# Seven block products in four of eight pairs, inner features in three parts, and low parts added by transfers: an encoder trunk on one core

## The chip, the cores and the metric

The kernel runs on one core of a Trainium2 chip. TensorE (PE in the profile; PEld is its weight load) multiplies, VectorE (DVE) and ScalarE (ACT) work elementwise, GpSimd (POOL) and SyncE (SP) issue transfers among other things. The metric is the device time of one execution in microseconds.

## The reference

Two layers over a sequence of 256 positions with 2048 features, in float32. Layer 0 mixes by a convolution module and a gating unit, layer 1 by a Fourier transform. Behind each stands the same feed-forward block, and these two blocks are where the change lies:

```
def swiglu(h, w_gate, w_up, w_down):
    return (jax.nn.silu(h @ w_gate) * (h @ w_up)) @ w_down

    h = rms_norm(x, ffn_norm_g[layer])
    x = x + swiglu(h, ffn_w_gate[layer], ffn_w_up[layer], ffn_w_down[layer])
```

`w_gate` and `w_up` are 2048 x 5632, `w_down` is 5632 x 2048.

## The kernel before

**Precision.** A product is done with operands in a rounded format (F32R) and each operand in two parts, a rounded high part and the rest. Weights come from HBM in chunks of 128 x 1024 (512 KB) into `raw` tiles. `parts_of` makes the two parts: ACT copies the chunk into the high part (L130), DVE subtracts that from the chunk (L131). A product takes three matmuls: high by high, high by low, low by high (`three`, L416).

**The feed-forward block.** The 5632 inner features are done in 11 groups of 512. `hidden_group` computes one group's gate and up values for both blocks of 128 positions, over the 16 feature tiles taken as eight pairs. `SEQ` says how a pair is done: "c" is the plain way, eight block products (24 matmuls of 512 columns); "s" is a scheme with seven products (21 matmuls) from sums of weights and of inputs. An "s" pair needs four prepared chunks out of two loaded ones (kinds "1122", "21", "sum", "sum2" in `load`), so it costs DVE additions (L161, L166, L167) besides the splits. `SEQ` is "ccscscsc", so a group has 5 x 24 + 3 x 21 = 183 matmuls. At the end of the last "s" pair ACT copies the shared sum `p1` out of PSUM (L461) and DVE forms the other sums (L462 to L465). `activate` then adds these to the plain sums, takes the sigmoid and multiplies.

The groups are done in two parts (`HALVES` = 6 and 5 groups). After each part the down projection adds that part's product to the residual `res`. For the group that has just ended, `turned` transposes the activations (L495): inside a part between the second and the third pair of the next group, at the end of a part after `PARTIAL` - 1 column tiles of the down projection have been done over the earlier groups.

**Order.** Each engine runs its instructions in the order in which the program has them after a scheduler has placed them. `Weights.chunk` prepares chunks ahead: as long as less than `AHEAD` units of PE work are prepared, it emits another. Small tasks (`activate` and the like) are emitted by ticks, one a chunk. The SP queue issues the loads in order, each once its `raw` tile is free. There are 5 `raw` tiles, 12 `part` tiles and 53 `op` tiles.

Of the kernel before, what the change touches and what calls it, by code (L numbers as in the profile page):

```python
# [22 lines left out]
F32 = mybir.dt.float32  # L23
# [5 lines left out]
P = 128  # L29
# [11 lines left out]
NG = D // GD  # L41
NV = CD // 512
CH = 8
AHEAD = 5
RAWS, PARTS = 5, 12
NOP = 53
HALVES = (6, 5)
SEQ = "ccscscsc"
PARTIAL = 3
NMISC = 3  # L50
PAIRS = 11
OPEN = 5
# [16 lines left out]

_ffn = []  # L70
for _g in HALVES:
    for _c, _ in ORDER * _g:
        _ffn += ["1122", "21", "sum", "sum2"] if _c == "s" else ["w", "w"]
    _ffn += ["w"] * (KD * 4 * _g // CH)
KINDS = (["w"] * ((4 * KD * KC + 2 * KC * KD) // CH) + _ffn + ["w"] * (KD * KD // CH) + _ffn)
UNITS = {"w": 2, "1122": 1, "21": 0.5, "sum": 1, "sum2": 1}
RMS_EPS = 1e-6
LN_EPS = 1e-5

# [11 lines left out]
def trunk(ctx, tc, xT, vec, sgu_gb, sgu_bs, sgu_wT, w, dft_c, dft_s, out):  # L91
# [27 lines left out]
    class Weights:  # L119
        def __init__(self):  # L120
            self.loaded, self.fetched, self.ahead, self.ready = 0, 0, 0, []
            self.tick, self.tasks, self.later, self.credit = 0, [], [], 0.0

        def parts_of(self, x, pieces=1):
# [18 lines left out]
        def load(self, pieces=1):  # L143
            kind = KINDS[self.loaded]
            h = slice(0, 512), slice(512, 1024)
            if kind == "w":
                r = self.parts_of(self.fetch(pieces), pieces)
            elif kind == "1122":
                self.pair = self.fetch(), self.fetch()
                r = self.parts_of(self.pair[0])  # L150
            elif kind == "21":
                x, t = self.pair[1], part()
                nc.scalar.copy(t[:, h[0]], x[:, h[1]])  # L153
                nc.vector.tensor_sub(t[:, h[1]], x[:, h[1]], t[:, h[0]].bitcast(F32))
                r = t,
            elif kind == "sum":

                t = self.sums = raws.tile([P, CH * P], F32, name="raw")
                two = lambda x: x.rearrange("p (o c) -> p o c", o=2)
                b12 = self.pair[1][:, h[0]].rearrange("p (o c) -> p o c", o=1).broadcast_to([P, 2, 512])  # L160
                nc.vector.tensor_add(two(t), two(self.pair[0]), b12)  # L161
                r = self.parts_of(t)
            else:

                t = raws.tile([P, CH * P], F32, name="raw")
                nc.vector.tensor_add(t[:, h[0]], self.sums[:, h[0]], self.pair[0][:, h[1]])  # L166
                nc.vector.tensor_add(t[:, h[1]], t[:, h[0]], self.pair[1][:, h[1]])  # L167
                r = self.parts_of(t)
            self.ahead += UNITS[kind]
            self.loaded += 1  # L170
            self.ready.append((kind, r))
# [23 lines left out]

        def chunk(self):
            while self.loaded < len(KINDS) and (not self.ready or
                                                self.ahead - UNITS[self.ready[0][0]] < AHEAD):
                self.load()
            self.step()  # L200
            kind, r = self.ready.pop(0)
            self.ahead -= UNITS[kind]
            return r
# [265 lines left out]
    def activate(norm, cs, sums, out):  # L469

        for b in range(NB):
            g, u = sums[2 * b:2 * b + 2]
            if b == 0:
                nc.vector.tensor_add(g, cs[0], g)  # L474
            else:
                nc.vector.tensor_sub(g, cs[2], g)
            nc.vector.tensor_add(u, cs[2 * b + 1], u)
        yield 1, 2.8
        for b in range(NB):
            g, u = sums[2 * b:2 * b + 2]  # L480
            r = norm.r[:, b:b + 1]
            sg = op(F32)
            nc.scalar.activation(sg, g, AF.Sigmoid, scale=r)  # L483
            nc.vector.scalar_tensor_tensor(g, g, r, sg, op0=ALU.mult, op1=ALU.mult)
            nc.vector.scalar_tensor_tensor(g, u, r, g, op0=ALU.mult, op1=ALU.mult)
            out.append(g)
        yield 1, 2.8

    def turned(h, hs, from_misc):

# [10 lines left out]
    def ffn(norm, after, last=False):  # L501
# [9 lines left out]
        for half, n in enumerate(HALVES):  # L511
# [13 lines left out]
                weights.start(activate(norm, cs, sums, h))  # L525
            k = 4 * (n - 1)
            accs = []
            for m in range(PARTIAL):
                if m == PARTIAL - 1:
                    turned(h, hs, True)  # L530
                accs.append(product(hs[:k], last=False))
            for m in range(KD):
# [1 line left out]
                    acc, = products(hs, 1)  # L534
                    nc.vector.tensor_add(res[:, m, :], res[:, m, :], acc)
                else:
                    x = residual(m, product(hs[k:], accs[m], first=False) if m < PARTIAL else product(hs))
                if final:
                    after(m, res[:, m, :])

# [79 lines left out]

    ys = []
    for j in range(KC):
        ys.append(op(F32, (P, S + 2 * PAD)))
        nc.gpsimd.memset(ys[j][:, :PAD], 0.0)
        nc.gpsimd.memset(ys[j][:, PAD + S:], 0.0)

# [4 lines left out]


    vs = [[[op() for _ in range(NV)] for _ in range(2)] for _ in range(NB)]
    vg = [[op(F32) for _ in range(NV)] for _ in range(NB)]
    st = small.tile([P, NB, NV, 6], F32, name="bnst")

    def gate_norm(nb, accs):
# [159 lines left out]
    weights.drain()  # L797

    n2 = Norm("mix1")
    ffn(n1, n2.add)  # L800


# [126 lines left out]
def _feed_forward(gate, up, down):  # L929
# [4 lines left out]
    for n in HALVES:  # L934
# [6 lines left out]
                chunks += [np.concatenate([t[:, g] for t in x], axis=1) for x in two]  # L941
        h = down[4 * g0:4 * (g0 + n)].transpose(2, 0, 1, 3)
        k = 4 * (n - 1)
        t = [h[:PARTIAL, :k], h[:PARTIAL, k:], h[PARTIAL:]]
        chunks += list(_chunks(np.concatenate([x.reshape(-1, P, P) for x in t])))
        g0 += n
    return np.stack(chunks)
# [63 lines left out]
```

## Time and profile before

| | |
|---|---|
| median of three runs | 1876.99 us (1874.48 to 1878.91) |
| the profiled execution | 1877.13 us, its span 1875.0 us |
| PE busy | 1849.9 us (99% of the span) |
| DVE busy | 1532.4 us (82%) |
| ACT busy | 1052.6 us (56%) |
| POOL busy | 19.8 us (1%) |

The span runs from the first to the last instruction of the program. A matmul's shown duration reaches beyond the start of the next, so PE's rate is read from the distance of starts, not from the mean duration. ACT, DVE and the transfers work beside PE, and a time of theirs counts only where PE waits for it.

### The profile page before, as it was taken

Reading aid. Unit: us, or ns where it says so; the run is one execution under the profiler, and the core shown is the slowest. Engines: PE = TensorE matmul, PEld = TensorE weight load, DVE = VectorE, ACT = ScalarE, POOL = GpSimd, SP = SyncE. Lnnn points to the kernel's source line nnn. Section 1 sums busy time; section 2 is a strip of 40 time slices with the busy share of each in tenths; the row PEclk is TensorE's granted clock in tenths of the full one; section 3 lists DMA queues with packets and bytes.
Section 4 is the critical chain, followed back from the end, with each engine's and each line's share of the span. In section 5 each row is a group of like instructions: output and inputs, shape, how many; then the busy total and the mean of one; then the engine's idle time right before and its main releaser. Section 6 shows DMA issues by size and latency. Waiting matters only on the chain.

```text
span 1875.0 us, 26253 instructions
## 1 busy us (share of the span) xinstructions
PE 1849.9 (99%) x9802; PEld 1584.6 (85%) x9802; DVE 1532.4 (82%) x2061; ACT 1052.6 (56%) x1444; POOL 19.8 (1%) x46
## 2 busy tenths in 40 slices
PE   8999999999999999999999999999999999999997
PEld 7989988878888888888888988888888888888886
DVE  7999969999997557899876678989997558999854
ACT  8988745555554335555555655555554335555642
POOL 1000000000000000000000000000000000000000
PEclk9999999999999999999999999999999999999999
DMA  7544553555557545555655264555556555555752
GB/s 269 174 165 151 180 191 135 185 197 202 180 205 251 188 164 181 180 196 197 242 196 185 70 212 147 191 183 205 205 208 222 190 169 180 191 188 200 252 188 83
DMA packets 98312, 351.38 MB, mean 187 GB/s; under 512 B 11268, under 2 KB 12420, under 8 KB 98184
## 3 DMA queue, kind: packets, MB, share of 16 engines
q1 hardware_dynamic: 97464, 347.73, 53.6%
q8 instruction: 77, 1.26, 0.3%
q10 hardware_dynamic: 720, 1.97, 0.3%
q14 instruction: 51, 0.42, 0.1%
HBM read 347.54 MB, written 2.10 MB: 186 GB/s over the span
## 4 chain that ended last, share of the span: by engine, by line
PE 86%; DVE 6%; DMA 4%; issue 2%; ACT 2%; SPq 0%; POOL 0%; POOLq 0%; DVEq 0%; ACTq 0%
PE acc L416 25%; PE acc L323 23%; PE m L416 13%; PE acc L324 12%; DMA raw<-in_w 4%; PE acc L333 2%; PE acc L334 2%; PE acc L335 2%; DVE part L131 1%; ACT part L130 1%; DVE raw L161 1%; PE acc L671 1%; PE acc L672 1%; PE acc L673 1%; DVE raw L166 1%
## 5 line engine op out<-in xcount | busy, mean ns | idle before, releaser
L130 ACT CAST part<-raw 128x1024 fp32r<-128x1024 f32 (+1 forms) x725 | 747.8, 1047 | 598.8 <-PE acc L323 288.1
L131 DVE TENSOR_TENSOR part<-raw,part 128x1024 fp32r<-128x1024 f32 (+1 forms) x725 | 872.3, 1219 | 242.1 <-ACT part L130 227.0
L323 PE MATMUL acc<-op,part 128*128 128x512 f32 x1900 | 664.0, 394 | 0.5 <-DVE op L343 0.5
L416 PE MATMUL acc<-part,op 128*128 128x512 f32 x2622 | 648.3, 391 | 0.9 <-ACT part L130 0.4
L416 PEld LDWEIGHTS acc<-part,op 128*128 128x128 f32 x2622 | 488.4, 188 | 108.3 <-ACT part L130 4.4
L324 PE MATMUL acc<-op,part 128*128 128x256 f32 x1900 | 531.9, 280 | 0.0
L323 PEld LDWEIGHTS acc<-op,part 128*128 128x128 f32 x1900 | 355.7, 187 | 82.1 <-DVE op L343 0.8
L416 PE MATMUL m<-part,op 128*128 128x512 f32 x1404 | 364.6, 391 | 0.5 <-DVE op L465 0.5
L324 PEld LDWEIGHTS acc<-op,part 128*128 128x128 f32 x1900 | 359.0, 189 | 0.5
L416 PEld LDWEIGHTS m<-part,op 128*128 128x128 f32 x1404 | 262.3, 188 | 56.9 <-DVE part L131 1.1
L333 PE MATMUL acc<-op,part 128*128 128x256 f32 x404 | 117.2, 290 | 6.5 <-ACT part L130 5.1
L335 PE MATMUL acc<-op,part 128*128 128x256 f32 x404 | 115.1, 286 | 1.2 <-DVE part L131 1.2
L334 PE MATMUL acc<-op,part 128*128 128x256 f32 x404 | 115.8, 287 | 0.0
L161 DVE TENSOR_TENSOR raw<-raw 128x1024 f32<-128x1024 f32 x66 | 80.7, 1222 | 10.7 <-DMA raw<-in_w 10.7
L333 PEld LDWEIGHTS acc<-op,part 128*128 128x128 f32 x404 | 78.6, 195 | 7.3 <-ACT part L130 5.5
L335 PEld LDWEIGHTS acc<-op,part 128*128 128x128 f32 x404 | 78.1, 194 | 1.9 <-DVE part L131 1.9
L334 PEld LDWEIGHTS acc<-op,part 128*128 128x128 f32 x404 | 78.8, 195 | 0.3 <-DVE op L232 0.2
L562 ACT ACTIVATE op<-op,vt 128x256 f32<-128x256 f32 x168 | 71.8, 499 | 0.0
L386 DVE TENSOR_TENSOR l<-acc,res 128x256 f32<-128x256 f32 x90 | 38.0, 423 | 32.0 <-PE acc L324 32.0
L153 ACT CAST part<-raw 128x512 fp32r<-128x512 f32 x66 | 41.1, 623 | 27.2 <-DMA raw<-in_w 12.2
L483 ACT ACTIVATE op<-op,is_r 128x512 f32<-128x512 f32 x44 | 31.9, 725 | 43.3 <-DVE op L474 33.1
L579 DVE TENSOR_TENSOR op<-op 128x512 f32<-128x512 f32 x80 | 54.1, 690 | 2.1 <-ACT op L562 1.8
(152 smaller groups left out, 1126.8 us busy)
## 6 DMA issues: line engine op xcount, KB each, us to landing
raw<-in_w SPq DMA_DIRECT2D x655, 512.0 KB, 4.3
res<-in_xT SPq DMA_DIRECT2D x7, 256.0 KB, 7.1
out<-res ACTq DMA_DIRECT2D x3, 512.0 KB, 2.8
raw<-in_w SPq DMA_DIRECT2D x4, 128.0 KB, 3.2
op<-in_sgu_wT SPq DMA_DIRECT2D x2, 256.0 KB, 4.9
raw<-in_dft_s SPq DMA_DIRECT2D x1, 512.0 KB
res<-in_xT SPq DMA_DIRECT2D x2, 128.0 KB, 2.2
raw<-in_dft_c SPq DMA_DIRECT2D x1, 256.0 KB, 2.8
```

The source lines that it names most:

```text
L130: nc.scalar.copy(hi[:, c], x[:, c])
L131: nc.vector.tensor_sub(lo[:, c], x[:, c], hi[:, c].bitcast(F32))
L153: nc.scalar.copy(t[:, h[0]], x[:, h[1]])
L161: nc.vector.tensor_add(two(t), two(self.pair[0]), b12)
L323: nc.tensor.matmul(acc, wh, x, start=first and k == 0, stop=False)
L324: nc.tensor.matmul(acc[:, :S], wl, x[:, :S], start=False, stop=last and k == len(xs) - 1)
L333: nc.tensor.matmul(acc, wh, x[:, :S], start=k == 0, stop=False)
L334: nc.tensor.matmul(acc, wh, x[:, S:], start=False, stop=False)
L335: nc.tensor.matmul(acc, wl, x[:, :S], start=False, stop=k == len(xs) - 1)
L416: nc.tensor.matmul(acc, x[f], wt[e], start=first and i == 0, stop=last and i == 2)
L562: nc.scalar.activation(t[:, f * S:(f + 1) * S], src, AF.Copy, scale=wc)
L579: nc.vector.tensor_add(sums, sums, t)
```

## The change

`SEQ` becomes "ccscsssc": four plain pairs, four with seven products. The parts are 4, 4 and 3 groups. In four of a group's eight plain chunks (`ADDED`, those of the third and fourth plain pair) the low part is made without DVE: ACT copies the chunk into the high part, writes the negative of the high part into the low part, and a transfer issued from POOL adds the chunk to it. `Silu` takes the place of sigmoid and one multiplication. The lead is 7 units from the first feed-forward block on; there are 7 `raw`, 14 `part` and 46 `op` tiles, and two sets of tiles of layer 0 move from `op` to `part` tiles.

```diff
-RAWS, PARTS = 5, 12
-NOP = 53
-HALVES = (6, 5)
-SEQ = "ccscscsc"
-PARTIAL = 3
+AHEAD, AHEAD_FFN = 5, 7
+RAWS, PARTS = 7, 14
+NOP = 46
+HALVES = (4, 4, 3)
+ADDED = (4, 5, 6, 7)
+SEQ = "ccscsssc"
+PARTIAL = lambda n: 3 if n > 3 else 4
...
+            elif kind == "added":
+
+                raw, hi, lo = self.fetch(), part(), part()
+                nc.scalar.copy(hi, raw)
+                nc.scalar.activation(lo, hi.bitcast(F32), AF.Copy, scale=-1.0)
+                nc.gpsimd.dma_start(lo, raw, accum_op=ALU.add)
+                r = hi, lo
...
-                                                self.ahead - UNITS[self.ready[0][0]] < AHEAD):
+                                                self.ahead - UNITS[self.ready[0][0]] < self.lead):
...
-            nc.scalar.activation(sg, g, AF.Sigmoid, scale=r)
-            nc.vector.scalar_tensor_tensor(g, g, r, sg, op0=ALU.mult, op1=ALU.mult)
-            nc.vector.scalar_tensor_tensor(g, u, r, g, op0=ALU.mult, op1=ALU.mult)
+            nc.scalar.activation(sg, g, AF.Silu, scale=r)
+            nc.vector.scalar_tensor_tensor(g, u, r, sg, op0=ALU.mult, op1=ALU.mult)
...
-            for m in range(PARTIAL):
-                if m == PARTIAL - 1:
+            for m in range(PARTIAL(n)):
+                if m == PARTIAL(n) - 1:
...
-        ys.append(op(F32, (P, S + 2 * PAD)))
+        if j % 3 == 0:
+            three_ys = wts.tile([P, 3, S + 2 * PAD], F32, name="part")
+        ys.append(three_ys[:, j % 3, :])
...
-    vg = [[op(F32) for _ in range(NV)] for _ in range(NB)]
+    vg = [wts.tile([P, NV, 512], F32, name="part") for _ in range(NB)]
+    vg = [[t[:, n, :] for n in range(NV)] for t in vg]
...
+    weights.lead = AHEAD_FFN
     ffn(n1, n2.add)
```

The first place is ACT at the end of a hidden group. Before, in the third group of the first block, its queue has these rows; L130 and L153 are copies into high parts, L461 is the copy of `p1`, and the rows behind it are the last chunk of the "s" pair and the chunks of the last plain pair and of the next group:

```order
L153 CAST part_4811<-raw_4799 128x512 [waits DMAHW1_49,PE_49,Activation_49]
L130 CAST part_4816<-raw_4814 128x1024 [waits DVE_49,PE_49,Activation_49]
L461 COPY op_4890<-acc_4691 128x512 [waits PE_49]
L130 CAST part_4823<-raw_4820 128x1024 [waits DVE_49,Activation_49]
L130 CAST part_4841<-raw_4839 128x1024 [waits DMAHW2_49,Activation_49]
L130 CAST part_4859<-raw_4857 128x1024 [waits DMAHW3_49,Activation_49]
L130 CAST part_4880<-raw_4878 128x1024 [waits DMAHW4_49,Activation_49]
L130 CAST part_4901<-raw_4899 128x1024 [waits DMAHW5_49,PE_49,Activation_49]
L130 CAST part_4919<-raw_4917 128x1024 [waits DMAHW6_49,PE_49]
```

In the changed kernel (its line numbers are other ones: L134 and L164 the copies, L472 the copy of `p1`, L155 and L156 the copy and the negation of an added chunk) the same place in the second group reads:

```order
L164 CAST part_4460<-raw_4448 128x512 [waits DMAHW1_49,PE_49,Activation_49]
L472 COPY op_4559<-acc_4349 128x512 [waits PE_49]
L134 CAST part_4468<-raw_4466 128x1024 [waits DVE_49]
L134 CAST part_4481<-raw_4478 128x1024 [waits DMASW3_49,DVE_49]
L155 CAST part_4493<-raw_4491 128x1024 [waits DMAHW2_49]
L156 ACTIVATE part_4494<-part_4493 128x1024 [waits Activation_49]
L155 CAST part_4509<-raw_4507 128x1024 [waits DMAHW3_49]
L156 ACTIVATE part_4510<-part_4509 128x1024 [waits Activation_49]
L134 CAST part_4528<-raw_4526 128x1024 [waits DMAHW4_49]
```

Two of the last "s" pair's copies now stand behind the copy of `p1` instead of one, and behind them the copy and negation of both chunks of the last plain pair, ahead of the next group's first chunk (`part_4528`). 17 of the 22 groups have these rows. In the other five (the first group of each later part, and of the second block) the two copies and the first L155 stand ahead of L472.

The second place is PE at the same end of a group. Before, in the second group, the last product into `p1` (`acc_4325`) is followed by 11 products and then these rows, in which the last plain pair (`part_4475`, `part_4476`) begins:

```order
L416 MATMUL acc_4327<-part_4450,op_4011 128x512
L416 MATMUL m_4205<-part_4457,op_3522 128x512 [waits Activation_49]
L416 MATMUL acc_4328<-part_4457,op_4010 128x512
L416 MATMUL acc_4203<-part_4475,op_3809 128x512 [waits Activation_49]
L416 MATMUL m_4205<-part_4458,op_3522 128x512 [waits DVE_49]
L416 MATMUL m_4205<-part_4457,op_3522 128x512
L416 MATMUL acc_4328<-part_4458,op_4010 128x512
L416 MATMUL acc_4328<-part_4457,op_4011 128x512
L416 MATMUL m_4204<-part_4475,op_3809 128x512
L416 MATMUL acc_4203<-part_4476,op_3809 128x512 [waits DVE_49]
```

In the changed kernel the rows are these; `part_4494` is the low part that a transfer completes (the wait on DMASW), `part_4528` the next group's first chunk. The row of `part_4528` with its wait on ACT is the 22nd after the last product into `p1`, the row with DMASW the 25th:

```order
L427 MATMUL acc_4352<-part_4481,op_4083 128x512
L427 MATMUL acc_4227<-part_4493,op_3802 128x512 [waits Activation_49]
L427 MATMUL m_4228<-part_4493,op_3802 128x512
L427 MATMUL m_4229<-part_4493,op_3802 128x512
L427 MATMUL m_4230<-part_4493,op_3802 128x512
L427 MATMUL acc_4604<-part_4528,op_3617 128x512 [waits Activation_49]
L427 MATMUL acc_4605<-part_4528,op_3617 128x512 [waits DVE_49]
L427 MATMUL acc_4606<-part_4528,op_3617 128x512 [waits DVE_49]
L427 MATMUL acc_4227<-part_4494,op_3802 128x512 [waits DMASW6_49]
L427 MATMUL acc_4227<-part_4493,op_3802 128x512
```

Four products with the high part and three of the next group now stand ahead of the first product with the low part, which waits for a transfer instead of DVE. In the 17 groups these distances are 22 or 23 and 24 to 26 (where a part ends, the 23rd is the down projection's first product), in the five 21 or 23 and 24 or 25. The second low part is waited for nine products further on. Over the program, the hidden groups have 180 products each in place of 183, POOL issues 88 such transfers, and ACT has one more activation table load, ahead of the first `Silu`. The down projection before has two column tiles of 4 x (n - 1) steps ahead of `turned` for a part of n groups (40 steps for six), and now two of 12 for four groups and three of 8 for three.

## Rows read from the trace of the kernel before

**Rows 1.** The page: busy time, share of the span, instructions
```profile
PE 1849.9 (99%) x9802; PEld 1584.6 (85%) x9802; DVE 1532.4 (82%) x2061; ACT 1052.6 (56%) x1444; POOL 19.8 (1%) x46
```

**Rows 2.** Groups by line: form, count, busy us, mean ns, idle
```profile
L416 PE MATMUL acc<-part,op 128*128 128x512 f32 x2622 | 648.3, 391 | 0.9 <-ACT part L130 0.4 <-DVE op L465 0.2
L131 DVE TENSOR_TENSOR part<-raw,part 128x1024 fp32r<-128x1024 f32 (+1 forms) x725 | 872.3, 1219 | 242.1 <-ACT part L130 227.0 <-PE acc L416 8.6 <-PE m L416 0.2
L130 ACT CAST part<-raw 128x1024 fp32r<-128x1024 f32 (+1 forms) x725 | 747.8, 1047 | 598.8 <-PE acc L323 288.1 <-DMA raw<-in_w 90.8 <-DVE raw L161 85.0
L161 DVE TENSOR_TENSOR raw<-raw 128x1024 f32<-128x1024 f32 x66 | 80.7, 1222 | 10.7 <-DMA raw<-in_w 10.7
L166 DVE TENSOR_TENSOR raw<-raw 128x512 f32<-128x512 f32 x66 | 45.5, 690 | 0.7
L484 DVE SCALAR_TENSOR_TENSOR op<-op,is_r 128x512 f32<-128x512 f32 x44 | 32.7, 751 | 0.0
L389 DVE TENSOR_TENSOR res<-acc,l 128x256 f32<-128x256 f32 x106 | 44.8, 424 | 2.6
L364 POOL TENSOR_TENSOR is_r<-is_v,mhalf 128x2 f32<-128x2 f32 x14 | 16.7, 1192 | 1844.9 <-DVE is_v L362 1844.9
L612 ACT ACT_TABLE_LOAD x2 | 2.6, 1283 | 0.0
```

**Rows 3.** Chain that ended last: start us, us, what
```profile
308.53 10.90 PE acc L416 x48
```

**Rows 4.** Timeline of PE, transposes after the second pair: start us, us
```profile
363.06 0.38 PE L495 MATMUL acc<-ident,op 128*128 128x128 f32 x2
494.21 0.44 PE L495 MATMUL m<-ident,op 128*128 128x128 f32 x2
1201.51 0.38 PE L495 MATMUL acc<-ident,op 128*128 128x128 f32 x2
1202.65 0.82 PE L495 MATMUL acc<-ident,op 128*128 128x128 f32 x6
1330.39 0.38 PE L495 MATMUL m<-ident,op 128*128 128x128 f32 x2
```

**Rows 5.** Timeline of ACT at the end of a group
```profile
864.67 0.59 ACT L461 COPY op<-acc 128x512 f32<-128x512 f32 x1 [2.48 <-PE acc L416]
865.15 2.94 ACT L130 CAST part<-raw 128x1024 fp32r<-128x1024 f32 x3
```

**Rows 6.** Waits: engine line <- releaser: us in total, times, longest
```profile
ACT op L461 <- PE acc L416: 21.1, 17, 3.0
```

**Rows 7.** Loads at L139; queue line; small transfers: count, KB, us to landing
```profile
DMA to landing us min/median/max: 2.6/4.3/7.9
q1 hardware_dynamic: 97464, 347.73, 53.6%
op<-op SPq DMA_DIRECT2D x8, 2.0 KB, 1.7
```

**Rows 8.** Windows on either side of the second normalization: busy times, PEclk
```profile
1028.00:1031.00 3.00, 1.51 (x12) 1.31 (x10) 2.27 (x4) 1.94 (x4) 0.00 (x0) 1.00 0.58 221
1031.00:1034.50 3.50, 3.50 (x18) 3.50 (x19) 3.11 (x9) 1.61 (x5) 0.74 (x1) 0.53 0.64 192
1034.50:1038.00 3.50, 3.50 (x30) 3.50 (x30) 1.36 (x3) 1.96 (x7) 0.00 (x0) 0.98 0.71 267
```

**Rows 9.** Timeline of PE there
```profile
1028.94 0.50 PE L370 MATMUL m<-oneD,ssq 128*128 128x2 f32 x4
1030.93 0.78 PE L370 MATMUL m<-oneD,sq 128*128 128x2 f32 x4 [1.49 <-ACT sq L254]
```

**Rows 10.** Timelines of PE and DVE after the first part's last group
```profile
568.06 0.28 PE L324 MATMUL acc<-op,part 128*128 128x256 f32 x1
572.30 0.28 PE L324 MATMUL acc<-op,part 128*128 128x256 f32 x1
576.90 1.41 DVE L485 SCALAR_TENSOR_TENSOR op<-op,is_r 128x512 f32<-128x512 f32 x2
```

More of the change, by code (lines that the diff above doesn't have):

```diff
@@ L43 @@
 CH = 8
-AHEAD = 5
-RAWS, PARTS = 5, 12
-NOP = 53
-HALVES = (6, 5)
-SEQ = "ccscscsc"
-PARTIAL = 3
+AHEAD, AHEAD_FFN = 5, 7
[5 more added lines that the diff above has]
+PARTIAL = lambda n: 3 if n > 3 else 4
 NMISC = 3
@@ L71 @@
 for _g in HALVES:
-    for _c, _ in ORDER * _g:
-        _ffn += ["1122", "21", "sum", "sum2"] if _c == "s" else ["w", "w"]
+    for _i, (_c, _) in list(enumerate(ORDER)) * _g:
+        _k = 2 * SEQ[:_i].count("c")
+        _ffn += (["1122", "21", "sum", "sum2"] if _c == "s" else
+                 ["added" if _k + _j in ADDED else "w" for _j in range(2)])
     _ffn += ["w"] * (KD * 4 * _g // CH)
 KINDS = (["w"] * ((4 * KD * KC + 2 * KC * KD) // CH) + _ffn + ["w"] * (KD * KD // CH) + _ffn)
-UNITS = {"w": 2, "1122": 1, "21": 0.5, "sum": 1, "sum2": 1}
+UNITS = {"w": 2, "added": 2, "1122": 1, "21": 0.5, "sum": 1, "sum2": 1}
 RMS_EPS = 1e-6
@@ L121, in __init__ @@
             self.loaded, self.fetched, self.ahead, self.ready = 0, 0, 0, []
+            self.lead = AHEAD
             self.tick, self.tasks, self.later, self.credit = 0, [], [], 0.0
@@ L482, in activate @@
             sg = op(F32)
-            nc.scalar.activation(sg, g, AF.Sigmoid, scale=r)
-            nc.vector.scalar_tensor_tensor(g, g, r, sg, op0=ALU.mult, op1=ALU.mult)
-            nc.vector.scalar_tensor_tensor(g, u, r, g, op0=ALU.mult, op1=ALU.mult)
+            nc.scalar.activation(sg, g, AF.Silu, scale=r)
+            nc.vector.scalar_tensor_tensor(g, u, r, sg, op0=ALU.mult, op1=ALU.mult)
             out.append(g)
-        yield 1, 2.8
+        yield 1, 1.4
     def turned(h, hs, from_misc):
@@ L536, in ffn @@
                 else:
-                    x = residual(m, product(hs[k:], accs[m], first=False) if m < PARTIAL else product(hs))
+                    x = residual(m, product(hs[k:], accs[m], first=False) if m < PARTIAL(n) else product(hs))
                 if final:
@@ L943, in _feed_forward @@
         k = 4 * (n - 1)
-        t = [h[:PARTIAL, :k], h[:PARTIAL, k:], h[PARTIAL:]]
+        m = PARTIAL(n)
+        t = [h[:m, :k], h[:m, k:], h[m:]]
         chunks += list(_chunks(np.concatenate([x.reshape(-1, P, P) for x in t])))
```

## Prediction

> **What bounds the kernel now.** I read the page first: PE has work for 99% of the span [rows 1], so what counts is the number of products and the moments at which PE waits. The chain of work that ended last gives a product's price: 48 products of 512 columns take 10.90 us [rows 3], 0.227 us each (the 391 ns in the groups by line [rows 2] reach into the next product). The timeline gives a hidden group's price by the transposes that each group has behind its second pair. Three groups lie between 363.06 and 494.21 and three between 1201.51 and 1330.39 [rows 4]: 43.7 us a group in the first block, 43.0 in the second. 183 products take 41.5, and eight transposes 0.9 (two more each time cost 0.11 a piece: x6 lasts 0.82, x2 lasts 0.38), 42.4 in all. So a group loses 1.3 and 0.6 us, at most 21 us over the 22 groups.
>
> Where PE loses that I read from ACT. In 17 of 22 groups ACT stands at L461 waiting for PE to finish `p1`, up to 3.0 us [rows 6]: ACT is ahead of its work, and yet everything behind the copy in its queue can't start before `p1` ends. The timeline shows it: after 2.48 us of idle time the copy starts, and 0.48 us later the casts follow [rows 5]. ACT's share (56%) and DVE's (82%) [rows 1] say little about this place; the order of ACT's queue after `p1` does.
>
> **What the change takes away.** Three products a group are 66 in all, 66 x 0.227 = 15.0 us. Of the 21 us of losses I take off 8, because the waits at the end of the groups are priced anew below and those elsewhere may stay (bounds 0 and 21).
>
> **What lies beside PE.** ACT gets four negations a group (4 x 1.05, the price of a cast [rows 2]) and the casts of a fourth "s" pair; DVE is relieved of four subtractions of 1.22 and two multiplications of 0.75 [rows 2], 6.4 us, and gets 4.5 for the fourth "s" pair (additions of 1.22, 0.69 and 0.69, one subtraction of 1.22 and half a one). Both stay below the time that a group takes, by the shares of [rows 1]. A third part brings 32 residual additions a block at 0.42 [rows 2], also DVE's. The table load takes 1.28 us of ACT once [rows 2]. I cost all these at nothing; what they hide behind is the products of the group. The layer 0 tiles that move to another pool likewise: nothing, give or take 2 us.
>
> **Part ends.** Before, 40 steps of the down projection stand between a part's last group and `turned`. Twelve of them lie between 568.06 and 572.30 [rows 10], so a step takes 0.353 us, and the 40 take 14.1; now there are 24, 8.5 us. The activations were ready about 10.5 us after the part's last group (567.8 to 576.90 + 1.41 [rows 10]); with one multiplication less for each block of positions, 1.4 us sooner: 9.1. So 0.6 us at six places, 3 us with rounding down (bounds 0 and, without the gain of `Silu`, 12).
>
> **The end of a group.** This decides. I count from the start of the last product into `p1`. It takes 0.39 [rows 2], then come ACT's copy (next start 0.48 later [rows 5]) and casts, whose starts lie 0.95 apart (three in 2.94, the last 1.05 long [rows 5]). By the order after the change, in 17 groups: first cast 0.87, second 1.82, high part of the first added chunk 2.77 to 3.82, its negation, which reads the high part, 3.82 to 4.87, second high part 4.77, its negation 5.82, and the next group's first cast only 6.77 to 7.82. PE wants that cast 22.5 products on, at 5.1 us, so **it waits 2.7 us however fast the transfers are**. It wants the low part 25 products on, at 5.67. With L from the issue of the transfer to PE, the low part is there at 4.87 + L, and the two waits overlap: the group loses the larger of 2.7 and L - 0.8. The second low part (6.87 + L, nine products later) asks for the same and adds nothing. In the five other groups the negation runs at 0.87 to 1.92, and the loss is 1.92 + L - 5.67 = L - 3.75.
>
> **The size of L.** No row shows such a transfer. It moves 512 KB as a load does; loads take 2.6 at the least, 4.3 in the median and 7.9 at most [rows 7], under traffic that shares the engines. It also has to read the other summand: 8 packets of 4 KB an engine, at 0.165 us each (53.6% of 16 engines' 1875 us over 97464 packets [rows 7]), 1.3 us. And POOL has to issue it: a small operation there takes 1.19 [rows 2]. That gives 2.6 + 1.3 + 1.2 = 5.1 by the quickest load and 6.8 by the median one. The lower bound is a tiny transfer inside the chip, 1.7 us [rows 7], with 1.3 us of packets and nothing for POOL: 3.0; the upper is the slowest load, 7.9 + 1.3 + 1.2 = 10.4. I take 5.7: nearer 5.1, since a 2-column operation on POOL is not a mere issue.
>
> Then 17 groups lose 4.9 each, 83.3 us, and five lose 1.95, 9.8 us.
>
> **The clock.** In the windows around the second normalization [rows 8] PE has only twelve matmuls within 3 us, eight of them of 2 columns, with 1.49 us of idle time between these [rows 9]; just behind that the granted clock falls to 0.53 of full speed, the lower of its two levels, for 3.5 us, which costs 0.47 x 3.5 = 1.6 us. A pause of 4.9 us, which is broken by a few products, resembles that. I let it cost 1.6 in half of the 17 groups, 14 us (bounds 0 and 27).
>
> **Sum.** Against the profiled execution, 1877.1 us (span 1875.0 and 2.1 around it; the median of the runs is 1877.0, the same): 1877.1 - 15.0 - 8 + 3 + 83.3 + 9.8 + 14 = **1964 us**, slower by 87.
>
> **The rivals.**
>
> *The transfer is quick (L up to 3.5).* Then only the next group's cast is waited for, 17 x 2.7 = 46 us. With little clock loss, 1877.1 - 15.0 - 8 + 46 = 1900, and 1890 to 1910 with the bounds of the vanished waits and of the part ends. For it: tiny transfers take 1.7. Against it: the engines carry loads more than half the time. Chance 0.18.
>
> The Trainium skill, "DMA: Bandwidth & Descriptors", section "Anatomy of one DMA — SWDGE (gpsimd) path", fits a transfer issued from GpSimd by 2.0 us and its bytes over 436 GB/s; for 512 KB that is an estimate of 3.2 us, and by it the time would be this rival's. No run here shows it, and the loads' median of 4.3 for the same bytes [rows 7] lies above it.
>
> *The transfer is slow (L of 8 and more).* The loads' longest times already reach 7.9 [rows 7] while DVE and the queue are busy, as they are at the end of a group. With L = 8: 17 x 7.2 + 5 x 4.25 = 144 us, and with the clock's 27, 1877.1 - 23 + 3 + 144 + 27 = 2028; the case spans 2005 to 2080 (the upper bound of L, 10.4, gives the end). Chance 0.18.
>
> The Trainium skill, "SBUF — State Buffer", section "SBUF: two separate sides", speaks for this one: a transfer issued from GpSimd can sit waiting while DVE holds the port that the two share, because its descriptors aren't written. No run here shows it.
>
> *Faster: PE doesn't stand still at the end of a group.* The saving of 23 us is used up once a group loses 23 / 22 = 1.05 us. For less, ACT's seven steps from `p1` to the next group's cast have to end by 6.2 us instead of 7.82, each one 0.23 us shorter, and L has to be under 1.85. For it: a negation reads and writes rounded numbers and may be quicker than the casts in the rows. Against it: two negations of no length at all take 2 us off the cast, but leave L, and the smallest transfer shown has 1.7. If it held in full, 1877.1 - 23 = 1854. Chance 0.06.
>
> *No change.* The gain and the waits cancel; the same mechanism at 1.05 us a group. Chance 0.02.
>
> **Range and chances.** The forecast's own case is L from 4 to 7. L = 4 gives 1877.1 - 23 + 17 x 3.2 + 5 x 0.25 = 1910, L = 7 with most of the clock's loss 1877.1 - 23 + 3 + 105 + 16 + 25 = 2003. It has the rest, 0.56. From 1890 to 2020 all of it and the quick transfer lie inside, and about a third of the slow one: 0.80. A difference of over 0.2% (3.8 us) is what runs of this kernel can tell. Faster has 0.06, the same 0.02, slower 0.92.
>
> **What would show it.** In the profile after, PE's idle time before the products of the feed-forward block should have two releasers that are almost absent now: the transfers of the added chunks, and ACT's plain cast, once a group, near its end; the waits should come in 17 long ones of about 5 us and five short ones. The new transfers' issue to landing should be 4 to 7 us. ACT should wait at the copy of `p1` (now L472) as before. The page's row of the granted clock should dip once a group where the pauses are long. Distances of transposes three groups apart should be near 3 x (40.9 + 0.9 + 4.9) = 140 us instead of 131.2 and 128.9 (where no part ends in between). The step that I doubt most is L; if PE's idle time at the added low parts is near nothing and the time still grows, the order of ACT's queue was right and L too large. If PE doesn't wait for ACT's cast either, the counting from `p1` is wrong, and the time falls.

## The result, and the profile after

The changed kernel takes 2023.45 us (median of 4 runs, 2019.97 to 2032.56) against 1876.51: the ratio is 1.0785 (95% interval 1.0764 to 1.0805), 147 us slower. The direction was forecast, the size was not: 1964 was predicted, and the time lies 3 us above the range. The profiled execution has a span of 2022.7 us.

The page of the changed kernel: the engines [rows 1], the queues of the transfers [rows 7], and the new transfers (KB each, us from issue to landing):

```profile
PE 1895.1 (94%) x9728; PEld 1596.2 (79%) x9728; DVE 1528.6 (76%) x2117; ACT 1151.6 (57%) x1579; POOL 94.8 (5%) x134
...
q1 hardware_dynamic: 97464, 347.73, 48.7%
q0 software_dynamic: 12672, 46.14, 12.1%
...
part<-raw POOLq DMA_DIRECT2D x88, 512.0 KB, 5.8
```

No engine became the bound by its share: ACT's busy time grew by 99 us and its share by one point, DVE's stayed, and PE's share fell. PE's busy time rose by 45 us although it has 66 products fewer, which points to a lower clock.

The view of cores (mean granted clock), and of the waits of the changed kernel (total us, times, longest):

```profile
core 0: 2022.7 us, clock 0.969
```

```profile
ACT op L494 <- DVE op L485: 116.1, 16, 7.8
...
DVE op L485 <- PE acc L427: 92.7, 17, 6.0
...
PE acc L427 <- DMA part<-raw: 70.1, 24, 4.3
ACT op L472 <- PE acc L427: 51.6, 21, 3.7
...
PE acc L427 <- ACT part L134: 22.3, 28, 1.5
...
PE acc L334 <- ACT part L134: 8.6, 6, 1.4
...
PE m L427 <- ACT part L134: 3.7, 16, 0.3
```

PE stands still for 70.1 us for the transfers and for 22.3 + 8.6 + 3.7 = 34.6 us for ACT's casts, 104.7 us together. The mean clock, 0.969 against 0.997 before, stands for 0.031 x 2022.7 - 0.003 x 1875 = 57 us. With the 15.0 us of products saved that is 104.7 + 57 - 15 = 147 us, as much as the difference of the spans (2022.7 - 1875.0 = 147.7). The sum closes because two inaccuracies of 12 us cancel. Some 12 us of the low clock fall into the waits themselves, where they cost nothing (0.79 over 3.4 us in the windows below, 17 times), so the clock costs about 45. And by the distance of starts each of the 74 waits is 0.16 us longer than shown (a product is shown with 0.39 and costs 0.227), so the waits cost about 116.

One group shows where. Its timeline on PE, from the transposes that begin it to those of the next group (start us, us, idle time before):

```profile
420.41 1.03 PE L505 MATMUL m<-ident,op 128*128 128x128 f32 x8
...
443.54 0.73 PE L427 MATMUL m<-part,op 128*128 128x512 f32 x2 [0.26 <-ACT part L134]
444.49 0.50 PE L427 MATMUL acc<-part,op 128*128 128x512 f32 x1 [0.21 <-ACT part L134]
...
449.49 0.50 PE L427 MATMUL acc<-part,op 128*128 128x512 f32 x1 [1.44 <-ACT part L134]
...
453.72 7.56 PE L427 MATMUL acc<-part,op 128*128 128x512 f32 x21 [3.27 <-DMA part<-raw]
...
471.10 1.03 PE L505 MATMUL acc<-ident,op 128*128 128x128 f32 x8
```

The group takes 50.7 us where its 180 products and eight transposes need 41.8; it loses 8.9. All of it lies at the end: short waits for the last "s" pair's casts, 1.44 for the next group's cast, 3.27 for the low part, and then 21 products that take 7.56 us instead of 4.9. The windows of that stretch (busy us of PE, PEld, DVE, ACT, POOL, then PEclk, DMA share, GB/s) say why these are slow, as [rows 8] do for one place of before:

```profile
446.00:450.30 4.30, 2.86 (x12) 1.86 (x11) 3.05 (x5) 4.27 (x6) 1.72 (x2) 1.00 0.98 281
450.30:453.70 3.40, 0.15 (x1) 0.00 (x0) 3.02 (x3) 1.98 (x3) 0.00 (x0) 0.79 1.07 219
453.70:459.40 5.70, 5.68 (x14) 4.47 (x15) 0.58 (x1) 0.00 (x0) 0.00 (x0) 0.53 0.84 266
459.40:465.00 5.60, 5.60 (x27) 4.60 (x26) 5.60 (x8) 2.89 (x4) 0.00 (x0) 1.00 0.38 145
```

While PE stands still the granted clock falls, and for 5.7 us behind the wait it stays near the lower of its two levels: 14 products where 27 fit into the next 5.6 us. The transfer engines are full (0.98 and 1.07) while the low part is under way. POOL's issues, and the transfers' time from issue to landing (min/median/max), are these for all 88; then the landing for the two of one third plain pair (issued from 369.6) and for the two of the last plain pair of the group shown (from 446.8), of which PE waits for the first, 6.9:

```profile
L157 POOL DMA_DIRECT2D part<-raw x88: 859/859/1042, 318.4 to 1930.4; - x88
DMA to landing us min/median/max: 4.5/5.8/8.0
...
DMA to landing us min/median/max: 5.1/5.4/5.7
...
DMA to landing us min/median/max: 6.9/7.1/7.4
```

The share of the engines doesn't tell the two places apart: in the third pair's window, 369.6 to 374.6, it is 0.98 too. The loads issued in the 6 us ahead differ, two there and four here; no run varies them alone:

```profile
L143 SPq DMA_DIRECT2D raw<-in_w x2: 327/328/328, 365.0 to 368.6; - x2
...
L143 SPq DMA_DIRECT2D raw<-in_w x4: 327/328/328, 442.2 to 445.9; - x4
```

One thing ties the groups together. DVE's L485 adds the sum into which the low part's products go, ACT's L494 (`Silu`) reads the result, and both stand in their engines' queues ahead of work for the next group:

```profile
409.07 0.72 ACT L494 ACTIVATE op<-op,is_r 128x512 f32<-128x512 f32 x1 [7.39 <-DVE op L485]
...
446.77 0.86 POOL L157 DMA_DIRECT2D part<-raw  x1 [23.24 <-ACT part L156]
...
458.82 0.69 DVE L485 TENSOR_TENSOR op<-acc,op 128x512 f32<-128x512 f32 x1 [5.50 <-PE acc L427]
...
459.55 0.72 ACT L494 ACTIVATE op<-op,is_r 128x512 f32<-128x512 f32 x1 [7.27 <-DVE op L485]
```

From L494 it is 37.7 us to the issue of the transfer, 7.0 more until PE uses the low part, 5.1 for the products at the low clock and 0.7 for L485: 50.5 us, the length of a group. A late low part holds ACT for 7.27 us, and that delays the chunks from which the next low part comes. This is read from the rows of one group; e18 below fits it.

### The profile page after: what moved, and what is told of

The parts are those of the page before. It is cut to its first block, busy times and chain, and to the rows that moved or that the text cites. A ratio compares the mean times of both kernels' runs of the same rounds, so it can differ in the third digit from the quotient of the medians.

```text
span 2022.7 us, 26508 instructions
## 1 busy us (share of the span) xinstructions
PE 1895.1 (94%) x9728; PEld 1596.2 (79%) x9728; DVE 1528.6 (76%) x2117; ACT 1151.6 (57%) x1579; POOL 94.8 (5%) x134
## 3 DMA queue, kind: packets, MB, share of 16 engines
q0 software_dynamic: 12672, 46.14, 12.1%
## 4 chain that ended last, share of the span: by engine, by line
PE 73%; DMA 10%; issue 9%; DVE 5%; ACT 2%; POOL 0%; SPq 0%; POOLq 0%; DVEq 0%; ACTq 0%
PE acc L334 22%; PE acc L427 19%; PE acc L335 11%; PE m L427 9%; DMA part<-raw 7%; DVE part L135 3%; DMA raw<-in_w 3%; PE acc L344 2%; PE acc L346 2%; PE acc L345 2%; DVE raw L177 1%; PE acc L684 1%; ACT part L134 1%; PE acc L685 1%; PE acc L686 1%
## 5 line engine op out<-in xcount | busy, mean ns | idle before, releaser
L134 ACT CAST part<-raw 128x1024 fp32r<-128x1024 f32 (+1 forms) x659 | 673.6, 1044 | 541.6 <-PE acc L334 284.5
L135 DVE TENSOR_TENSOR part<-raw,part 128x1024 fp32r<-128x1024 f32 (+1 forms) x659 | 792.8, 1217 | 212.0 <-ACT part L134 177.0
L427 PE MATMUL acc<-part,op 128*128 128x512 f32 x2568 | 679.7, 405 | 93.1 <-DMA part<-raw 70.1
L334 PEld LDWEIGHTS acc<-op,part 128*128 128x128 f32 x1908 | 357.8, 188 | 97.7 <-ACT part L134 11.1
L427 PE MATMUL m<-part,op 128*128 128x512 f32 x1392 | 385.2, 403 | 4.0 <-ACT part L134 3.7
L335 PEld LDWEIGHTS acc<-op,part 128*128 128x128 f32 x1908 | 359.9, 189 | 0.6
L157 POOL DMA_DIRECT2D part<-raw x88 | 76.0, 863 | 1547.5 <-ACT part L156 1246.3
L172 DVE TENSOR_TENSOR raw<-raw 128x1024 f32<-128x1024 f32 x88 | 107.3, 1219 | 6.1 <-DMA raw<-in_w 6.1
L156 ACT ACTIVATE part<-part 128x1024 fp32r<-128x1024 f32 x88 | 93.3, 1060 | 11.5 <-PE acc L427 5.3
L494 ACT ACTIVATE op<-op,is_r 128x512 f32<-128x512 f32 x44 | 31.8, 722 | 116.1 <-DVE op L485 116.1
L155 ACT CAST part<-raw 128x1024 fp32r<-128x1024 f32 x88 | 91.5, 1040 | 8.6 <-PE acc L427 8.6
L485 DVE TENSOR_TENSOR op<-acc,op 128x512 f32<-128x512 f32 x22 | 15.2, 690 | 92.7 <-PE acc L427 92.7
L344 PEld LDWEIGHTS acc<-op,part 128*128 128x128 f32 x396 | 77.5, 196 | 8.5 <-ACT part L134 6.3
L397 DVE TENSOR_TENSOR l<-acc,res 128x256 f32<-128x256 f32 x122 | 51.0, 422 | 41.9 <-PE acc L335 41.8
L345 PEld LDWEIGHTS acc<-op,part 128*128 128x128 f32 x396 | 77.7, 196 | 0.4 <-DVE op L243 0.3
```

The lines of the kernel that those rows point to most:

```text
L134: nc.scalar.copy(hi[:, c], x[:, c])
L135: nc.vector.tensor_sub(lo[:, c], x[:, c], hi[:, c].bitcast(F32))
L155: nc.scalar.copy(hi, raw)
L156: nc.scalar.activation(lo, hi.bitcast(F32), AF.Copy, scale=-1.0)
L157: nc.gpsimd.dma_start(lo, raw, accum_op=ALU.add)
L334: nc.tensor.matmul(acc, wh, x, start=first and k == 0, stop=False)
```

## The experiments

Ratios are against the kernel before on the same chip, with 95% intervals.

| run | us | ratio |
|---|---|---|
| e5, copy of `p1` behind the casts | 2040.4 | 1.086 (1.083 to 1.089) |
| e2, no added low parts | 1892.1 | 1.008 (1.006 to 1.010) |
| e7, the same, copy behind | 1901.7 | 1.013 (1.011 to 1.015) |
| e6, before, copy behind | 1884.4 | 1.003 (1.002 to 1.005) |
| e3, added in the third plain pair | 1915.6 | 1.021 (1.019 to 1.023) |
| e4, added in the last plain pair | 1991.1 | 1.061 (1.058 to 1.063) |
| e9, order ccsscssc | 2048.8 | 1.092 (1.088 to 1.096) |
| e13, the same, copy behind | 2043.0 | 1.088 (1.086 to 1.091) |
| e18, 20 fill products a group | 1969.1 | 1.049 (1.048 to 1.051) |
| e19, no sums | 1861.7 | 0.992 (0.991 to 0.993) |
| e17, order of before, no added | 1870.0 | 0.997 (0.996 to 0.998) |
| e21, order of before, added | 1894.8 | 1.010 (1.008 to 1.011) |
| e23, negated, DVE adds | 1959.2 | 1.044 (1.042 to 1.045) |
| e15, before with Silu | 1871.9 | 0.997 (0.996 to 0.998) |
| e16, before in three parts | 1881.8 | 1.002 (1.001 to 1.003) |
| e27, no added, two sums on POOL | 1964.9 | 1.047 (1.044 to 1.050) |
| e28, added, two sums on POOL | 2018.0 | 1.076 (1.074 to 1.079) |

### Is it the copy of `p1` in ACT's queue? (e5, e2, e7, e6)

The theory of the prediction: what stands behind `p1` on ACT comes too late. The rival: the transfers, or the kernel's other new parts.

```diff
-                    nc.scalar.copy(a, p1)
+                    tc.keep_in_program_order(nc.scalar.copy(a, p1))
```

That is e5, and for the kernel before e6. e2 has `ADDED = ()`, e7 both.

> The changed kernel with one edit: the copy of p1 is pinned on ACT behind what the program has emitted ahead of it (the casts and negations of the last plain pair and two casts of the next group), in all 22 groups. The 88 transfers stay. Theory, the order of ACT's queue is the cause: casts and negations no longer start only when p1 ends, so the transfers start several us sooner, the waits at the end of a group (about 111 us in the changed kernel, of which 2.8 a group for ACT's casts and 3.4 to 4.6 for the transfer) and the stretches of low clock behind them (about 55 us) go: 1850 to 1880 us. Rival, transfers issued from POOL are too slow beside the loads wherever they stand: at least 50 us of waits for transfers stay, over 1930 us.

> The changed kernel without added low parts (DVE subtracts in all chunks); the fourth seven-product pair, three parts, lead, pools and Silu stay, and so does the copy of p1 ahead of the casts. Theory: behind p1 stand five casts up to the next group's first, ready at 0.87 + 4 x 0.95 + 1.05 = 5.7 us; PE wants it at about 5, so 0.5 to 1.5 us a group are lost, and some clock: 1865 to 1895 us. Rival, the transfers cost little and the three parts or the fourth seven-product pair lose the time: over 1950 us.

> The run without added low parts, and with the copy of p1 pinned behind the casts. Theory: nothing is left of the waits at the end of a group; the 66 products saved are seen, 15 us, and part of the 8 to 11 us that the kernel before loses in its groups: 1850 to 1865 us. Rival, DVE is now short (a fourth seven-product pair is 4.5 us more of DVE a group): 1875 us or more with PE waiting for DVE.

> The kernel before with the copy of p1 pinned behind the casts that the program emits ahead of it, nothing else. Theory: its hidden groups lose 12 us, of which half or more stand at the end of a group behind p1: 1865 to 1873 us. Rival, the copy's place costs the kernel before nothing: within 0.2% of 1877 us.

e2 came as expected: without the added parts 131 of the 147 us are gone. The other three did not. With the copy out of the way e5 is no faster than the changed kernel but 17 us slower (15 by the ratios), and PE waits 110.0 us for transfers instead of 70.1. The theory in its first form fell. In e5's trace ACT stands at the second of these casts, now for DVE's sum (L178):

```profile
PE acc L427 <- DMA part<-raw: 110.0, 22, 7.3
```

```profile
446.05 0.69 DVE L178 TENSOR_TENSOR raw<-raw 128x512 f32<-128x512 f32 x1
...
447.10 1.04 ACT L134 CAST part<-raw 128x1024 fp32r<-128x1024 f32 x1 [0.67 <-DVE raw L178]
```

The changed kernel's own trace shows why, in DVE's queue at the same group's end:

```profile
431.96 1.22 DVE L172 TENSOR_TENSOR raw<-raw 128x1024 f32<-128x1024 f32 x1
...
437.34 2.36 DVE L135 TENSOR_TENSOR part<-raw,part 128x1024 fp32r<-128x1024 f32 x2 [1.16 <-ACT part L134]
...
440.22 1.22 DVE L172 TENSOR_TENSOR raw<-raw 128x1024 f32<-128x1024 f32 x1
441.47 0.69 DVE L177 TENSOR_TENSOR raw<-raw 128x512 f32<-128x512 f32 x1
442.20 0.69 DVE L178 TENSOR_TENSOR raw<-raw 128x512 f32<-128x512 f32 x1
```

and ACT's queue beside it:

```profile
428.61 2.00 ACT L134 CAST part<-raw 128x1024 fp32r<-128x1024 f32 x2 [3.00 <-DVE raw L178]
...
433.26 1.06 ACT L134 CAST part<-raw 128x1024 fp32r<-128x1024 f32 x1 [2.13 <-PE acc L427]
436.26 2.00 ACT L134 CAST part<-raw 128x1024 fp32r<-128x1024 f32 x2 [1.94 <-DVE raw L178]
...
441.96 0.59 ACT L472 COPY op<-acc 128x512 f32<-128x512 f32 x1 [3.18 <-PE acc L427]
442.44 1.99 ACT L134 CAST part<-raw 128x1024 fp32r<-128x1024 f32 x2
...
445.42 1.06 ACT L156 ACTIVATE part<-part 128x1024 fp32r<-128x1024 f32 x1
```

By the view ACT waits 3.18 us for PE at the copy, and it does so 21 times in the program (51.6 us). But the two casts behind the copy need DVE's sums: L172 ends at 441.44 and L178 at 442.89, only then can the second cast run (443.4 in the row). Without the copy ACT would gain half a microsecond. Two queues were late by nearly the same amount, and the view shows the one that came last (so also at 433.26, where the row names PE and DVE's L172 had ended at 433.18). The casts after DVE's L178 are 436.26 - 428.61 = 7.65 us apart: ACT and DVE, each waiting for the other, need that for one "s" pair, and PE consumes it in 21 x 0.227 = 4.8. By these rows three in a row cost 8.6 us of what is prepared ahead.

e6 and e7 show that the pinned copy is itself a loss of 6 to 10 us. In e5 ACT's wait for PE moved to another place: by its view of waits ACT stands 77 us at L352, behind PE's transposes (L505), where the changed kernel has 13. The waits for `p1` [rows 6] cost the kernel before nothing that a later copy gives back.

### Which of the transfers? (e3, e4)

`ADDED = (4, 5)` and `ADDED = (6, 7)`: the third or the last plain pair alone.

> The changed kernel with added low parts only in the third plain pair (44 transfers instead of 88); the last plain pair's low parts are DVE's again. If the place decides (behind p1, where nothing is prepared ahead): these 44 transfers are hidden as they are in the changed kernel, and the time is that of the run without added parts or a little less, 1880 to 1895 us. If each transfer costs (traffic, POOL, ACT's negation): half of the 131 us between the two runs, about 1955 us.

> The changed kernel with added low parts only in the last plain pair (the other 44 transfers). If the place decides: all of the loss stays, 2005 to 2035 us. If each transfer costs: about 1955 us.

Against e2 the third pair's 44 cost 23 us, the last pair's 99. The place decides the larger part, but "hidden in the third pair" was wrong for e3: PE waits there for transfers of that pair, nearly as long as the 23 us (in the changed kernel its waits for transfers all stand at the last pair). The view of waits of e3, and the landing times of e3 and then e4 (min/median/max):

```profile
PE acc L427 <- DMA part<-raw: 22.4, 13, 2.1
```

```profile
DMA to landing us min/median/max: 4.5/5.0/6.8
```

```profile
DMA to landing us min/median/max: 5.5/6.9/8.8
```

### Is it three "s" pairs in a row? (e9, e13, e19)

```diff
-SEQ = "ccscsssc"
+SEQ = "ccsscssc"
```

> The changed kernel with the order of pairs ccsscssc, so that two seven-product pairs stand ahead of the last plain pair instead of three; all 88 transfers stay, two of the group's added pairs are still the third and the last plain one. The copy of p1 still stands ahead of the last pair's casts in 18 groups. If the queue of ACT alone sets the loss: as the changed kernel, 2005 to 2035 us. If three seven-product pairs in a row use up what is prepared ahead (DVE's work for one takes about 6.7 us and PE's 4.8): the loss shrinks, under 1980 us.

> The run with the order ccsscssc, and with the copy of p1 pinned on ACT behind the casts and negations that the program emits ahead of it. If two limits lie on top of each other, ACT's queue and the work used up by three pairs in a row, lifting both shows what lifting either does not: transfers start earlier, waits and low clock mostly go, 1860 to 1910 us. If neither is it (the part tiles, the loads, the transfers themselves): 1980 us or more.

Both came out slower than the changed kernel. "Three in a row" is not the point. A reading that fits, though no run shows it alone: two, an added pair and two use up as much, since each "s" pair lacks nearly 3 us and the added pair's 4 us of ACT stand in the same chain. In e13 PE waits 107.5 us for transfers, in 41 places instead of 24: the third pair's are waited for too. So the length of the chain itself had to be changed. e19 leaves out the sums:

```diff
...
-                nc.vector.tensor_add(two(t), two(self.pair[0]), b12)
-                r = self.parts_of(t)
+                r = self.parts_of(self.pair[0])
...
-                nc.vector.tensor_add(t[:, h[0]], self.sums[:, h[0]], self.pair[0][:, h[1]])
-                nc.vector.tensor_add(t[:, h[1]], t[:, h[0]], self.pair[1][:, h[1]])
-                r = self.parts_of(t)
+                r = self.parts_of(self.pair[1])
```

> The changed kernel with DVE's three additions of each seven-product pair left out (the sum chunks are replaced by the two loaded chunks, which are split as before; two raw tiles less are used a pair): 2.6 us less of DVE a pair, and ACT no longer waits for them. All 88 transfers and their places stay; the copy of p1 now comes behind the added chunks on ACT. If what is prepared ahead is lost in the chain between DVE's additions and ACT's casts over three such pairs in a row: the transfers start earlier and PE's waits for them mostly go, 1860 to 1920 us. If the transfers are too slow with any lead: over 1980 us.

1861.7 us, with all 88 transfers, their negations and their places: 162 us less than the changed kernel, 15 less than the kernel before, about the worth of the 66 products (what e17 wins further below, 6 us, stands in it too). PE's waits for transfers in this run, and ACT's rows at the end of a group, where it now waits only for PE:

```profile
PE acc L419 <- DMA part<-raw: 0.5, 1, 0.5
```

```profile
416.74 1.05 ACT L134 CAST part<-raw 128x1024 fp32r<-128x1024 f32 x1 [0.47 <-PE m L419]
...
419.46 1.06 ACT L155 CAST part<-raw 128x1024 fp32r<-128x1024 f32 x1 [0.30 <-PE acc L419]
```

A transfer of 5 to 7 us is hidden whole once the chunks are prepared ahead. The edit also frees two raw tiles a pair and brings the copy behind the casts; e5 shows that moving the copy alone gains nothing; the raw tiles were not tried alone. Against them speaks that ACT and DVE wait only 22 us for loads in the whole changed kernel (15.2 + 6.1 + 0.6 by its view of waits) and 79 in e19 (53.6 + 25.5), which lost nothing by it.

### Is the rest the clock? (e18)

```diff
+FILL = 20
...
+    zero = const.tile([P, P], F32R, name="zero")
...
+                    if i == len(ORDER) - 1 and x is xa:
+                        for _ in range(FILL):
+                            nc.tensor.matmul(cs[0], zero, parts[0][:, :512], start=False, stop=False)
```

> The changed kernel with 20 useless products a group (a zero operand against the high part of the last plain pair's first chunk, added to a gate sum) ahead of the first product with an added low part: 440 products, 100 us of PE work, which stand where PE waits for the transfer. They also keep the next group's products from standing there, and the copy of p1 comes behind the added chunks on ACT, so the run with the copy behind the casts (2040 us) is the nearest one. If the low clock behind the wait comes from PE's standing still: the stretches of half speed (about 55 us in all) mostly go, and the time is 1975 to 2010 us despite the added work. If it has another cause: 2040 us or more.

```profile
core 0: 1966.7 us, clock 0.996
```

```profile
PE acc L432 <- DMA part<-raw: 3.4, 2, 2.3
```

```profile
445.58 4.83 PE L451 MATMUL acc<-part,zero 128*128 128x512 f32 x20
450.25 6.08 PE L432 MATMUL acc<-part,op 128*128 128x512 f32 x26
```

100 us of useless products make the kernel 54 us faster, 6 more than the expected range allowed. The clock is back at 0.996, 26 products behind the fill take 6.08 us, the full rate, and the waits for transfers fall to 3.4 us. The last was not expected in this measure: the fill takes up the waiting time, and because the products behind it are quick, what follows (DVE's L485 and ACT's L494, which wait for the group's last products) starts sooner, and with it the next group's chain. ACT's wait at L494 (L502 there) falls from 116.1 us to 4.7. The copy of `p1` also moves, behind the first negation in 14 of the 22 groups; in the group shown it stands ahead of both as in the changed kernel, and the products behind the fill run at the full rate all the same.

### Transfer or negation? (e23, e21, e17)

```diff
-                nc.gpsimd.dma_start(lo, raw, accum_op=ALU.add)
+                nc.vector.tensor_add(lo, raw, lo.bitcast(F32))
```

> The changed kernel with ACT's copy and negation of the added chunks in their places, but with DVE's addition (1.2 us) in place of the 88 transfers. If the transfer's 7 us at the last plain pair are the loss: what is left lies near the run with DVE's plain low parts, 1892 to 1910 us. If ACT's negations (4.2 us a group in the chain between ACT and DVE) are a good part of it: 1930 us or more.

1959.2: of the 131 us between e2 and the changed kernel 67 come with ACT's negation and the addition behind it (e2 has the copy too), 64 with the transfer in DVE's place. ACT's share of busy time (57%) hid that: its work is in series with DVE's, not beside it.

e17 is e2, and e21 the changed kernel, with `SEQ = "ccscscsc"`.

> The changed kernel with the order of pairs of before (ccscscsc, three seven-product pairs, 183 products a group) and without added low parts: what is left of the change is three parts, the lead, the pools and Silu. If the fourth seven-product pair in its place is what loses the time in the run without added parts (1892 us): at most 1877 us, without the 15 us that the 66 products save. If the three parts or the pools lose it: 1890 us or more.

> The same with the 88 added low parts, which now belong to the third and fourth of five plain pairs; each is followed by a seven-product pair, and the last plain pair is DVE's. If transfers are hidden wherever work is prepared ahead: within 15 us of the run with this order and without them. If ACT's negations and the transfers cost by themselves: 30 us or more above it.

e17 is faster than both kernels. Between "s" pairs stand plain pairs, in which the chain catches up, and PE waits for no cast of a group. The fourth "s" pair, meant to save 15 us, costs 22 (e2 against e17). The added parts cost 25 us in this order too, though no wait for a transfer stands among PE's larger ones; the expectation put 30 us as the mark of a cost by themselves, so this lies between the two. By the views of waits ACT and DVE wait 191 us for loads in e21 and 6 in e17, and PE waits 12.6 us for DVE's sums behind `p1` (L474, L476): here the added parts seem to reach the chain through the loads.

### What the other parts are worth (e15, e16)

> The kernel before with Silu alone: one multiplication of 0.75 us less for each block of positions, 1.5 us of DVE a group, and one table load. If DVE's chain sets what the groups of before lose (12 us): some of it is won back, 1868 to 1874 us. If not, within 0.2% of 1877 us.

> The kernel before with the groups in three parts of 4, 4 and 3 and the column tiles ahead of the transposes that go with it, nothing else. By the prediction's part ends: 24 steps of 0.353 us in place of 40 cover 9.1 to 10.5 us, so up to 2 us are lost at each of six places, 1877 to 1889 us. If the extra residual additions and the shorter cover cost nothing: within 0.2% of 1877 us.

`Silu` alone wins 0.28% (5 us), the three parts lose 0.22% (4 us), and the rest of e17 (the lead and the pools) wins about 5 us, by difference; it was not run alone. So e15 is the change's useful part in one line, and as fast as e17.

### A shorter chain without leaving work out (e27, e28)

The two half-chunk sums of each "s" pair go to POOL (`nc.gpsimd.tensor_add` at L177 and L178).

> The run without added low parts (1892 us), with the two half-chunk additions of each seven-product pair given to POOL (1.2 us less of DVE a pair, but the cast of that chunk now waits for POOL, whose time for such an addition no run has shown). If DVE's length in the chain is what counts and POOL is not much slower than DVE's 0.69 us: 1860 to 1885 us. If POOL takes more than about 1.5 us for each: as before that edit or slower, 1892 to 1960 us.

> The changed kernel with the same two additions on POOL, all 88 transfers in place. By the same condition: with a quick POOL the last plain pair's chunks come earlier and part of the 147 us is won back, 1930 to 2000 us; with a slow one 2023 us or more.

The groups by line of e27 show POOL's price (DVE's is 0.69 [rows 2]):

```profile
L178 POOL TENSOR_TENSOR raw<-raw 128x512 f32<-128x512 f32 x88 | 183.7, 2087 | 6.9
L177 POOL TENSOR_TENSOR raw<-raw 128x512 f32<-128x512 f32 x88 | 144.9, 1646 | 1206.3 <-DVE raw L172 548.0 <-DVE part L135 479.2 <-DMA raw<-in_w 95.5
```

3.7 us in place of 1.4 in the chain: e27 loses 73 us against e2, 5 more than the expected range allowed. That a longer chain costs again is in line with e19; e28, with both, is 5 us faster than the changed kernel and not slower, so there the slower sums were made up by something that these runs don't name.

## Why the prediction came out low

147 us were lost where 87 were forecast. By the sums above some 23 us of the difference are longer waits (116 against 93), 31 the clock (45 against 14) and 8 the waits of before that did not vanish; 3 forecast for the part ends did not show. So the places were right, in 17 long waits and five short ones as forecast. Two sizes, the clock and L, were too small, and the cause that was named for the waits was wrong.

- **Products saved, 15.0 us.** Right, within some 6 us: e19, which has the 180 products and hardly a wait, is 15 us below the kernel before.
- **The end of a group, casts.** 2.7 us were forecast for the next group's cast alone. That wait is 1.44 in the row; with the short waits ahead of it (0.26, 0.21 and several below what the view prints), at the last "s" pair's casts, it is about 2.8 by the distances of the products. That the sum agrees is luck. The count of ACT's steps came true (the negation ends at 446.48, 4.5 us after the copy's start, as forecast), and that too by luck, because DVE's sums come at nearly the same moment as the copy. Wrong was the cause: the step that all follows from "everything behind the copy in its queue can't start before `p1` ends" held DVE for free ("what lies beside PE"). e5 refutes the copy as the cause, e19 shows the chain of ACT and DVE. The new work that was costed at nothing, since each engine's share leaves room, is the cause: the fourth "s" pair's sums and the four negations stand in one chain, and this chain waits once a group for PE.
- **The size of L.** 5.7 was taken, from the end of the negation. In the group shown it is 453.72 - 446.48 = 7.2, with 0.3 ahead of the issue and 6.9 to landing, behind four loads; the held-up casts release raw tiles together, which would explain the four. With 7.2 the 17 groups lose 6.4 instead of 4.9, 26 us more, and the group's waits are about 6.2. The rival "slow transfer" (L = 8: 2028 us) came nearest. The five short waits came as forecast (9.8 us; 1.64 to 2.35 each in the trace).
- **The Trainium skill**, "DMA: Bandwidth & Descriptors", section "Anatomy of one DMA — SWDGE (gpsimd) path": its estimate of 3.2 us for 512 KB doesn't agree with these transfers, whose quickest took 4.5; the measurement decides. The rule of the Trainium skill, "SBUF — State Buffer", section "SBUF: two separate sides", on DVE holding up descriptors is tied there to DVE operations that use two ports, which the prediction left out; it is not visible here: POOL's issue took 0.86 us in the median and 1.04 at most.
- **The clock.** 14 us were taken and about 45 measured (57 with what falls into the waits), above the upper bound of 27. The fall in [rows 8, 9] was the right model, but it comes behind each of the 17 long waits, not half of them, and costs 0.47 x 5.7 = 2.7 us in the group shown instead of 1.6; 17 times that is 46, near the 45. This is the term that was most wrong; e18 confirms its cause.
- **Part ends, 3 us.** e16 measured 4 us, by the whole change to three parts. In the changed kernel no wait of this kind shows.
- **What would show it.** PE's two releasers, the transfers and ACT's casts, are those that were named. The group shown takes 50.7 us, where 46.7 was forecast (140 for three).
- **Waits of before that vanish, 8 us.** e17 wins 6.5 with three parts and `Silu` in it. The kernel before has hardly a wait of PE for a cast in its groups, so what the distances of transposes showed there was not waits, and nothing of it could vanish with them.

## What to carry to other kernels

Work that two engines hand to each other is costed as one chain, not against each engine's busy share: here two engines busy for 57% and 76% kept PE waiting. When a wait is removed by reordering a queue, look at what the next instructions in it wait for on the other engine before counting the gain. A wait on TensorE can cost more than its length: here waits of 3 to 4 us cost another 2.7 us each by the low clock behind them. And look for the way back: here the product that waited for the transfer held up the work from which the next transfer came.

## What the runs showed of the hardware

- Behind a wait of 3.27 us the granted clock was 0.53 for 5.7 us in the group shown (14 products instead of 27); 440 idle-filling products of 100 us in all brought the mean clock from 0.969 back to 0.996, and the kernel was 54 us faster.
- A transfer issued from POOL that adds 512 KB in the chip to a tile took 4.5 to 8.0 us to land (5.1 and 5.7 where two loads had been issued in the 6 us ahead, 6.9 and 7.4 where four had); its packets took 0.31 us of an engine each (12.1% of 16 x 2022.7 us over 12672), twice a load's.
- POOL took 1.65 and 2.09 us in the mean for a 128x512 addition in float32 (e27) that DVE does in 0.69.

Open: why pinning the copy costs the kernel before 6 us, how the 25 us of e21 divide between negations and transfers, and what of e19's gain more free raw tiles would bring alone.
